# One layer of a hybrid decoder on one core: the second half of x read already turned, row roots and C A^t sums moved from GpSimd to VectorE, the last chunk's stores moved to ScalarE's queue

## The chip, the cores and the metric

The kernel runs on one core of one Trainium2 chip. The core has five engines that work beside each other, each through its own instruction queue in order: TensorE (PE; its weight loads are shown as PEld), VectorE (DVE), ScalarE (ACT), GpSimd (POOL) and SyncE (SP), which does no arithmetic and issues most DMAs. ACT issues some DMAs too. An instruction that waits for a semaphore holds up all that stands behind it in the same queue; a queue's own entries are shown as SPq, ACTq and so on.

The metric is device microseconds (us) of one execution. Lower is better.

## The reference

One layer (DEPTH = 1) over 2048 tokens of width 1024, in float32:

```
h = rms_norm(x, norm1_g)
proj = h @ w_in                       # columns shared by three mixers
o_a = swa_sink_mixer(qa, ka, va)      # attention, window 128
o_b = s5_mixer(u)                     # complex diagonal state space, 512 columns u of proj
o_c = nsa_mixer(qc, kvc, gates)       # compressed, selected and window attention
x = x + rms_norm_each(o_a, o_b, o_c) @ w_out
x = x + relu(rms_norm(x) @ w_up)**2 @ w_down
```

The RMS norm divides each row of x by the root of its mean square. The kernel applies this factor after the product, row by row, and the gain norm1_g to the weights. Of s5_mixer only one thing matters here: for each of 32 groups the kernel needs C A^t for t = 0 to 16, a complex product whose two halves are multiplied apart and summed.

## The kernel before, in words

The kernel is five stages behind each other: the front (norm, w_in, the state space), attention A beside the GLU of the state space, the sparse attention with the output product, the up projection and the down projection. The change lies in the front (`phase_front`, the first 420 us).

**Rows.** The 2048 tokens are cut into 16 row tiles s = 0 to 15 of 128 tokens each (tokens s, s + 16, ...). The host hands x over as it is. `fetch(s)` (L101) loads tile s, 128x1024 float32 or 512 KB, on SP's queue. `load_h(s)` (L106) turns it in: eight transposes of 128x128 on PE (L116), four to a PSUM tile pt with two buffers; ACT casts pt to float32r (hh, L118), DVE makes the remainder hl = pt - hh (L119). `scale()` (L121) squares x in place on ACT with a sum (L123) and takes the reciprocal root of the sum on POOL by `rsqrt_into`, eight instructions on 128x1 (L44 to L49: two to start, three rounds of two). This factor r is called the row root below. Tile s of x has three buffers; hh and hl have eight, so row tiles 8 to 15 take the place of 0 to 7.

**Products.** A `chunk` is the product of eight row tiles (half 0: s = 0 to 7; half 1: s = 8 to 15) with one slice of w_in: a, b, c (384, 384 and 396 columns) and u, v (256 columns each, together the state space's u). One row's `product` (L155) is 24 matmuls: eight steps of three, high by high, low by high, high by low (L76 to L78), into one of two PSUM accumulators pm. For u and v ACT evicts pm to u_st with the row root as scale (L172). For a, b, c ACT evicts to a row buffer po (L176), squares the heads (L178), DVE sums them (L179), and the row is stored to memory (L180) on SP's queue, one row late (`store(1)`). Weights come on SP's queue (L133) and are split by ACT (L141) and DVE (L142).

**Order around the change.** A first list of steps does half 0 of a. A second one merges half 0 of b, c and u with `ssm_tables`, which makes the tables of the state space; its last PE work is the turning of C (p, L452). The third one (L236 to L244) is where the change lies: half 0 of v, half 1 of v, half 1 of u, 24 products; after every second entry from the third on one `turn_in(s)` for s = 8 to 15 is inserted (load_h, scale, and the fetch of s + 3); x8 to x10 are fetched ahead of it; and this list is merged with the 17 steps of `pair_steps`. A fourth one does half 1 of a, b and c (each row in two parts) merged with `ssm_steps`, the scan. Then the next stage begins, with its weights (graw, L626) and bias tables (Ts, T).

**Pairs.** Step b of `pair_steps` makes C A^t for two groups: oCA = AR * C1 on POOL (L483), ot = AI * C2 on DVE (L484, one buffer), and the sum oCA + ot on POOL (L485). Then for the pair before: its oCA is stored (L489), two small products pk on PE (L493), and kst, with one buffer, is filled by DVE (L496) and ACT (L497) and stored (L498).

The lists give the order of the program. A planner beneath places each instruction on its engine's queue from that order and from when it expects it to be ready: the trace shows fetches of the second half at 35.77 to 45.76 us, long before their place in the lists. Memory of a pool that has been closed can be given to a later pool, whose first use then waits for the last use of the earlier one.

Of the kernel before, what the change touches and what calls it, by code (L numbers as in the profile page):

```python
# [7 lines left out]
F32 = mybir.dt.float32  # L8
# [8 lines left out]
P = 128  # L17
# [39 lines left out]
def rsqrt_into(nc, pool, y, ss, scale, n, tag, eng=None):  # L57
    h = pool.tile([P, n], F32, tag=tag + "h", name=tag + "h")
    t = pool.tile([P, n], F32, tag=tag + "t", name=tag + "t")
    rsqrt_steps(eng or nc.vector, y, ss, h, t, scale)  # L60
# [17 lines left out]
    nc.tensor.matmul(out, sl, mh, start=False, stop=last)  # L78


def phase_front(tc, C, x, norm1_g, w_in, u_st, pd, rh_a, prm, dkp, dca, pre, extra, done):

    nc = tc.nc
    with ExitStack() as ctx:
# [11 lines left out]
        pdv = {kind: t.rearrange("(c s) e -> s c e", s=T16) for kind, t in pd.items()}  # L96
        wv = w_in[0].rearrange("(k p) n -> p k n", p=P)
        g1 = sm.tile([P, NK], F32, tag="g1", name="g1", bufs=1)
        r_of, raw_x, hs = {}, {}, {}

        def fetch(s):  # L101
            if s < T16:
                raw_x[s] = xp.tile([P, D], F32, tag="x", name=f"x{s}", bufs=3)
                nc.sync.dma_start(raw_x[s], xv[s])

        def load_h(s):  # L106
            xt = raw_x.pop(s)
            p = hp[s % 8 == 7]
            hh = p.tile([P, NK, P], F32R, tag="hh", name=f"hh{s}")
            hl = p.tile([P, NK, P], F32R, tag="hl", name=f"hl{s}")  # L110
            hs[s] = hh, hl
            for half in range(2):
                pt = ps_t.tile([P, 4, P], F32, tag="pt", name=f"pt{s}_{half}")
                for j in range(4):
                    k = 4 * half + j
                    nc.tensor.transpose(pt[:, j], xt[:, k * P:(k + 1) * P], C["ident"])  # L116
                sl = slice(4 * half, 4 * half + 4)
                nc.scalar.copy(hh[:, sl], pt)  # L118
                nc.vector.tensor_tensor(hl[:, sl], pt, hh[:, sl], op=ALU.subtract)  # L119

            def scale():  # L121
                ss = xp.tile([P, 1], F32, tag="ss", name=f"ss{s}")
                nc.scalar.activation(xt, xt, AF.Square, accum_out=ss)  # L123
                r = r_of[s] = sm.tile([P, 1], F32, tag="r", name=f"r{s}", bufs=T16)
                rsqrt_into(nc, xp, r, ss, 1.0 / D, 1, "rq", nc.gpsimd)
            return scale

        def raw_w(ch, q, m, pool, bufs):
# [26 lines left out]
        def product(s, W, ch, k0=0, k1=NK, between=()):  # L155
            kind, c0, n = ch
            hh, hl = hs[s]
            if k0 == 0:
                open_[s, ch] = ps_m.tile([P, n], F32, tag="pm", name=f"pm{s}_{kind}{c0}")
            pm = open_[s, ch]  # L160
            between = list(between)
            for k in range(k0, k1):
                mm3(nc, pm, hh[:, k], hl[:, k], W[k][0], W[k][1], k == 0, k == NK - 1)
                if between:
                    between.pop(0)()
            if k1 < NK:
                return
            if kind == "u":
                r = T16 - 1 - s
                g0 = (c0 - 512) // 16  # L170
                dst = u_st[:, g0:g0 + 16, (r // 8) * P + (r % 8) * 16:(r // 8) * P + (r % 8) * 16 + 16]
                nc.scalar.activation(dst, pm.rearrange("p (g q) -> p g q", q=16), AF.Copy, scale=r_of[s])  # L172
            else:
                f, nh, step = HEADS[kind]
                o = sp.tile([P, n + nh], F32, tag="po", name=f"po{s}_{kind}", bufs=3)
                nc.scalar.activation(o[:, 0:n], pm, AF.Copy, scale=r_of[s])  # L176
                sq = sp.tile([P, 6, 64], F32, tag="sq", name=f"sq{s}_{kind}", bufs=1)[:, 0:nh]
                nc.scalar.activation(sq, o[:, f:f + nh * step].rearrange("p (h d) -> p h d", d=step)[:, :, 0:64], AF.Square)  # L178
                nc.vector.tensor_reduce(o[:, n:n + nh], sq, axis=AX.X, op=ALU.add)  # L179
                rows.append(lambda: nc.sync.dma_start(pdv[kind][s], o))  # L180
                store(1)

        rows = []
# [50 lines left out]
        run(merge(body, [lambda: next(gen, None)] * TABLE_PARTS))  # L234
        pairs = pair_steps(tc, C, S, dkp, dca, pre, ps_g)
        body = chunk(ch_v, 0, W[0, ch_v], []) + chunk(ch_v, 1, W[0, ch_v], steps[1, ch_u]) + chunk(ch_u, 1, W[1, ch_u], steps[1, ch_a])  # L236
        for s in range(8, 11):
            fetch(s)
        for s in range(8, T16):
# [2 lines left out]
                fetch(s + 3)  # L242
            body.insert(2 * (s - 8) + 3, turn_in)
        run(merge(body, pairs))  # L244
        done()
        tp = ctx.enter_context(tc.tile_pool(name="sg", bufs=2))
        c_b = chunk(ch_b, 1, W[1, ch_b], steps[1, ch_c], 2)
# [224 lines left out]
def pair_steps(tc, C, S, dkp, dca, tp, ps):  # L472

    nc = tc.nc
    M = {}
    NB = G // GB

    def outer(b):
        bc = [P, GB, 17, 16]
        CA = M[b] = tp.tile(bc, F32, tag="oCA", name=f"oCA{b}", bufs=2)  # L480
        t1 = tp.tile(bc, F32, tag="ot", name=f"ot{b}", bufs=1)
        ar, ai = (S[n][:, :, group_slice(b)].rearrange("p t g -> p g t").unsqueeze(3).broadcast_to(bc) for n in ("AR", "AI"))
        nc.gpsimd.tensor_tensor(CA, ar, S["C1"][:, group_slice(b)].unsqueeze(2).broadcast_to(bc), op=ALU.mult)  # L483
        nc.vector.tensor_tensor(t1, ai, S["C2"][:, group_slice(b)].unsqueeze(2).broadcast_to(bc), op=ALU.mult)  # L484
        nc.gpsimd.tensor_tensor(CA, CA, t1, op=ALU.add)  # L485

    def local(b):
        CA = M.pop(b)
        nc.sync.dma_start(dca[b], CA)  # L489
        pk = ps.tile([P, GB, 256], F32, tag="pb", name=f"pk{b}", bufs=2)  # L490
        for i in range(GB):
            g = b * GB + i
            nc.tensor.matmul(pk[:, i], S["Yp"][:, g:g + 8].rearrange("p a b -> p (a b)"), CA[:, i, 0:16].rearrange("p a b -> p (a b)"),  # L493
                             start=True, stop=True)
        kst = tp.tile([16, GB, 256], F32, tag="kst", name=f"kst{b}", bufs=1)
        nc.vector.tensor_tensor(kst[:, :, 0:16], pk[0:16, :, 0:16], S["dD"][:, group_slice(b)], op=ALU.add)  # L496
        nc.scalar.copy(kst[:, :, 16:256], pk[0:16, :, 16:256])  # L497
        nc.sync.dma_start(dkp[group_slice(b), :, 112:368].rearrange("g q c -> q g c"), kst)  # L498

    return [lambda b=b: (b < NB and outer(b), b and local(b - 1)) for b in range(NB + 1)]  # L500
# [1318 lines left out]
                w = nw  # L1819


def trunk(tc, x, norm1_g, w_in, qk_g, sinks, rel_bias, a_re, a_im, log_dt, b_re, b_im, c_re, c_im, d_skip, glu_w, glu_b,
          cmp_pos, cmp_w1, cmp_w2, out_norm_g, w_out, norm2_g, w_up, w_down,
          k_ident, k_anti, k_ramp, k_oh2, k_ohs, k_blk, k_forced, k_wmask, k_rows31, out, dbg=None):
    nc = tc.nc
    with ExitStack() as ctx:
# [9 lines left out]
        def late_loads(tp, ps):  # L1836
# [7 lines left out]
            for j in (0, 2):  # L1844
# [17 lines left out]
        u_st = up.tile([P, G, 256], F32, name="u_st")  # L1862
        c_pre = c_all.enter_context(ExitStack())
        pre = c_pre.enter_context(tc.tile_pool(name="pre", bufs=1, side="right"))
        phase_front(tc, C, x, norm1_g, w_in, u_st, pd, rh_a, (a_re, a_im, log_dt, b_re, b_im, c_re, c_im, d_skip), dkp, dca,
                    pre, late_loads, c_pre.close)
        c_b = c_all.enter_context(ExitStack())
        bp = c_b.enter_context(tc.tile_pool(name="bp", bufs=1, reuse_waits="tile"))
# [90 lines left out]
```

## Time and profile before

| | us |
|---|---|
| median of 3 runs | 2546.9 (2543.54 to 2548.43) |
| profiled execution | 2552.13 |
| its span | 2550.2 |
| PE busy | 2444.3 (96%) |
| DVE busy | 1721.8 (68%) |
| ACT busy | 1324.6 (52%) |
| POOL busy | 1203.2 (47%) |

The profile is of one execution. A group or a row names the line of the kernel (L116), the engine, the operation, out<-in by the program's names without buffer numbers, and partitions x elements. In an order of time the first two columns are the start and the length in us, and in brackets stands the idle time of the engine before it and what ended it. Rows of one kind that follow each other are merged (x8). Matmuls are pipelined and their ends are modelled, so starts say more than lengths. A row of the waits reads: who waited, for whom, us in total, times, longest.

The stages by time: half 0 of the products until about 163 us, the rows 8 to 15 turned in from 163 to 209, the rest of u until 240, the fourth list until 417, then the other stages.

### The profile page before, as it was taken

The page shows a single profiled execution, that of the slowest core. Times are in us where ns is not written, and L with a number is a line of the kernel's source. Part 1 is how long each engine was busy: PE and PEld are TensorE (multiplying, and loading weights), DVE is VectorE, ACT ScalarE, POOL GpSimd, SP SyncE. Part 2 cuts the span into 40 slices and gives each one's busy share as a digit, 9 for nine tenths or more (in the row PEclk, how much of TensorE's full clock was granted, in tenths as well). Part 3 has the DMA queues.
Part 4 walks back from the last instruction along what each step waited for, and adds up shares of the span by engine and source line. Part 5 has one row for each costly group of instructions (what it writes and reads, how often), then busy time and mean ns, then how long its engine had stood idle before and what let it go on. Part 6 is the DMA issues. An engine that isn't in the chain of part 4 may idle for free.

```text
span 2550.2 us, 38303 instructions
## 1 busy us (share of the span) xinstructions
PE 2444.3 (96%) x12776; PEld 2065.4 (81%) x12776; DVE 1721.8 (68%) x3424; ACT 1324.6 (52%) x2767; POOL 1203.2 (47%) x1263
## 2 busy tenths in 40 slices
PE   8999999899989999899999999999999999999999
PEld 8989997677778878788778787788887888888887
DVE  4743884775587787677554545745457888888886
ACT  6334545675576566555455555654554444334442
POOL 3045222223445354454646666666554444545447
PEclk9999999998999999999999999999999999999999
DMA  6153425311121112131656677755547534444335
GB/s 200 61 127 96 125 87 163 97 58 49 44 92 51 57 51 68 55 98 55 198 193 189 191 198 210 227 160 155 148 121 261 164 102 126 133 132 132 120 101 197
DMA packets 397174, 324.65 MB, mean 127 GB/s; under 512 B 51974, under 2 KB 363916, under 8 KB 395152
## 3 DMA queue, kind: packets, MB, share of 16 engines
q1 hardware_dynamic: 360880, 297.03, 39.2%
q10 hardware_dynamic: 36096, 25.17, 3.1%
q8 instruction: 101, 1.65, 0.3%
q14 instruction: 97, 0.79, 0.1%
HBM read 209.66 MB, written 112.45 MB: 126 GB/s over the span
## 4 chain that ended last, share of the span: by engine, by line
PE 63%; DVE 5%; DMA 3%; POOL 3%; issue 3%; ACT 2%; SPq 0%; ACTq 0%; DVEq 0%; POOLq 0%
PE pdc L1755 7%; PE pdb L1755 7%; PE pda L1755 7%; PE pub L1566 6%; PE puc L1566 6%; PE pua L1566 6%; PE pdd L1755 3%; PE pud L1566 3%; PE poc L911 3%; PE pps L900 2%; PE pw L76 2%; PE pw L77 2%; PE pw L78 2%; PE pqs L876 1%; PE pqs L877 1%
## 5 line engine op out<-in xcount | busy, mean ns | idle before, releaser
L1420 ACT CAST v<-vr 128x512 fp32r<-128x512 f32 x224 | 139.4, 624 | 305.4 <-DMA vr<-vd 142.9
L1421 DVE TENSOR_TENSOR v<-vr,v 128x512 fp32r<-128x512 f32 x224 | 233.7, 1052 | 78.2 <-ACT v L1420 77.9
L1755 PE MATMUL pdc<-dw,v 128*128 128x512 f32 x768 | 187.4, 393 | 4.1 <-ACT dw L1420 3.2
L1755 PE MATMUL pda<-dw,v 128*128 128x512 f32 x768 | 184.5, 389 | 0.0
L1755 PE MATMUL pdb<-dw,v 128*128 128x512 f32 x768 | 184.5, 389 | 0.0
L1537 POOL TENSOR_TENSOR fs<-ur,ur 128x512 f32<-128x512 f32 x64 | 92.9, 1452 | 176.4 <-DMA ur<-in_w_up 131.2
L1755 PEld LDWEIGHTS pdc<-dw,v 128*128 128x128 f32 x768 | 145.5, 190 | 35.8 <-ACT dw L1420 3.6
L1755 PEld LDWEIGHTS pdb<-dw,v 128*128 128x128 f32 x768 | 144.2, 188 | 30.0
L1755 PEld LDWEIGHTS pda<-dw,v 128*128 128x128 f32 x768 | 144.1, 188 | 30.0
L1421 DVE TENSOR_TENSOR ul<-ur,uh 128x512 fp32r<-128x512 f32 x96 | 93.3, 972 | 109.8 <-ACT uh L1420 109.7
L1421 DVE TENSOR_TENSOR ul<-fs,uh 128x512 fp32r<-128x512 f32 x128 | 133.7, 1048 | 33.9 <-ACT uh L1420 33.9
L1420 ACT CAST uh<-fs 128x512 fp32r<-128x512 f32 x128 | 78.2, 621 | 141.7 <-PE pub L1566 56.4
L887 POOL TENSOR_SCALAR sls<-sls,dens,gt 128x128 f32<-128x128 f32 (+15 forms) x64 | 81.7, 1277 | 105.8 <-DVE dens L886 85.7
L903 ACT CAST ths<-pps 128x512 fp32r<-128x512 f32 (+1 forms) x144 | 79.8, 560 | 79.6 <-PE poc L911 58.1
L904 DVE TENSOR_TENSOR tls<-pps,ths 128x512 fp32r<-128x512 f32 (+1 forms) x144 | 93.8, 658 | 38.7 <-ACT ths L903 34.1
L76 PE MATMUL pw<-wo_h,mh 128*128 128x512 f32 x256 | 109.7, 428 | 7.6 <-ACT mh L1250 5.8
L900 PE MATMUL pps<-c_ident,sls 128*128 128x128 f32 x544 | 103.0, 281 | 9.1 <-POOL sls L887 5.4
L1582 POOL TENSOR_TENSOR ev<-e,e 128x512 f32<-128x512 f32 x64 | 98.3, 1535 | 27.9 <-ACT e L1579 16.8
L887 POOL TENSOR_SCALAR slw<-slw,denw,gt 128x640 f32<-128x640 f32 (+4 forms) x64 | 52.9, 827 | 122.1 <-DVE denw L886 98.5
L78 PE MATMUL pw<-wo_h,ml 128*128 128x512 f32 x256 | 105.0, 411 | 2.1 <-DVE ml L1251 2.1
L77 PE MATMUL pw<-wo_l,mh 128*128 128x512 f32 x256 | 106.4, 416 | 0.0
L1566 PE MATMUL puc<-fh,uh 128*128 128x512 f32 x256 | 101.0, 395 | 5.3 <-DVE eu L1575 5.3
(562 smaller groups left out, 7960.6 us busy)
## 6 DMA issues: line engine op xcount, KB each, us to landing
vr<-vd SPq DMA_DIRECT2D x224, 256.0 KB
ur<-in_w_up SPq DMA_DIRECT2D x128, 256.0 KB
vd<-ev SPq DMA_DIRECT2D x128, 256.0 KB
vd<-e ACTq DMA_DIRECT2D x64, 256.0 KB
dr<-in_w_down SPq DMA_DIRECT2D x32, 512.0 KB
x<-in_x SPq DMA_DIRECT2D x16, 512.0 KB
mx<-in_x SPq DMA_DIRECT2D x16, 512.0 KB
x<-mx ACTq DMA_DIRECT2D x16, 512.0 KB
```

The lines of the kernel that those rows point to most:

```text
L76: nc.tensor.matmul(out, sh, mh, start=first, stop=False)
L77: nc.tensor.matmul(out, sh, ml, start=False, stop=False)
L78: nc.tensor.matmul(out, sl, mh, start=False, stop=last)
L887: nc.gpsimd.tensor_scalar(x, x, den[:, h:h + 1], gate, op0=ALU.mult, op1=ALU.mult)
L900: nc.tensor.transpose(pt[:, j, hh], sls[hh][:, (b0 + j) * P:(b0 + j + 1) * P], C["ident"])
L904: nc.vector.tensor_tensor(tl[:, 0:nb], pt[:, 0:nb], th[:, 0:nb], op=ALU.subtract)
L1420: nc.scalar.copy(dh, src)
L1421: nc.vector.tensor_tensor(dl, src, dh, op=ALU.subtract)
L1537: nc.gpsimd.tensor_tensor(t, x, y, op=op)
L1566: nc.tensor.matmul(bank[b], w[:, k], h[o][:, k], start=first and k == 0 and n == 0, stop=k == HALF - 1 and n == 2, skip_group_check=True)
L1582: nc.gpsimd.tensor_tensor(tile_("v" + o), x, y, op=op)
L1755: nc.tensor.matmul(bank[b, q], x[:, q, j], y[:, j], start=first and j == 0 and n == 0, stop=j == 1 and n == 2, skip_group_check=True)
```

## The change

Four edits:

1. For s = 8 to 15 the host hands over a second input x_t with the tiles already turned. `fetch` loads it (xt, 512 KB, three buffers) ahead of x, and `load_h` casts from it in SBUF; the transposes and pt are not used for these rows. x itself is still loaded, for the square, now with two buffers in place of three.
2. Both lie in a new pool a_x2, opened after the tables and closed ahead of `done()`.
3. The row root of s = 8 to 15 and the sum of C A^t in every pair are on DVE in place of POOL.
4. The stores of chunk c for s = 8 to 15 are issued by ACT in place of SP.

```
         def fetch(s):
             if s < T16:
-                raw_x[s] = xp.tile([P, D], F32, tag="x", name=f"x{s}", bufs=3)
+                if s >= 8:
+                    turned_x[s] = late_p[0].tile([P, NK, P], F32, tag="xt", name=f"xt{s}", bufs=3)
+                    nc.sync.dma_start(turned_x[s], xt_in[s - 8])
+                raw_x[s] = (late_p[0] if s >= 8 else xp).tile([P, D], F32, tag="x", name=f"x{s}", bufs=2 if s >= 8 else 3)
                 nc.sync.dma_start(raw_x[s], xv[s])
...
-                pt = ps_t.tile([P, 4, P], F32, tag="pt", name=f"pt{s}_{half}")
-                for j in range(4):
-                    k = 4 * half + j
-                    nc.tensor.transpose(pt[:, j], xt[:, k * P:(k + 1) * P], C["ident"])
                 sl = slice(4 * half, 4 * half + 4)
+                if s >= 8:
+                    pt = turned_x[s][:, sl]
+                else:
+                    pt = ps_t.tile([P, 4, P], F32, tag="pt", name=f"pt{s}_{half}")
+                    for j in range(4):
+                        k = 4 * half + j
+                        nc.tensor.transpose(pt[:, j], xt[:, k * P:(k + 1) * P], C["ident"])
                 nc.scalar.copy(hh[:, sl], pt)
                 nc.vector.tensor_tensor(hl[:, sl], pt, hh[:, sl], op=ALU.subtract)
...
-                rsqrt_into(nc, xp, r, ss, 1.0 / D, 1, "rq", nc.gpsimd)
+                rsqrt_into(nc, xp, r, ss, 1.0 / D, 1, "rq", nc.vector if s >= 8 else nc.gpsimd)
...
-                rows.append(lambda: nc.sync.dma_start(pdv[kind][s], o))
+                rows.append(lambda: (nc.scalar if s >= 8 and kind == "c" else nc.sync).dma_start(pdv[kind][s], o))
...
+        c_x = ctx.enter_context(ExitStack())
+        late_p.append(c_x.enter_context(tc.tile_pool(name="a_x2", bufs=1)))
         for s in range(8, 11):
             fetch(s)
...
         run(merge(body, pairs))
+        c_x.close()
         done()
...
-        nc.gpsimd.tensor_tensor(CA, CA, t1, op=ALU.add)
+        nc.vector.tensor_tensor(CA, CA, t1, op=ALU.add)
...
+            host["x_t"] = _np.asarray(inputs[n])[0].reshape(P, T16, NK, P).transpose(1, 3, 2, 0)[8:]
```

More of the change, by code (lines that the diff above doesn't have):

```diff
@@ L78, in mm3, with phase_front @@
     nc.tensor.matmul(out, sl, mh, start=False, stop=last)
-def phase_front(tc, C, x, norm1_g, w_in, u_st, pd, rh_a, prm, dkp, dca, pre, extra, done):
+def phase_front(tc, C, x, xt_in, norm1_g, w_in, u_st, pd, rh_a, prm, dkp, dca, pre, extra, done):
     nc = tc.nc
@@ L98, in phase_front @@
         g1 = sm.tile([P, NK], F32, tag="g1", name="g1", bufs=1)
-        r_of, raw_x, hs = {}, {}, {}
+        r_of, raw_x, turned_x, hs, late_p = {}, {}, {}, {}, []
         def fetch(s):
             if s < T16:
-                raw_x[s] = xp.tile([P, D], F32, tag="x", name=f"x{s}", bufs=3)
+                if s >= 8:
+                    turned_x[s] = late_p[0].tile([P, NK, P], F32, tag="xt", name=f"xt{s}", bufs=3)
+                    nc.sync.dma_start(turned_x[s], xt_in[s - 8])
+                raw_x[s] = (late_p[0] if s >= 8 else xp).tile([P, D], F32, tag="x", name=f"x{s}", bufs=2 if s >= 8 else 3)
                 nc.sync.dma_start(raw_x[s], xv[s])
@@ L1819, in phase_down, with trunk @@
                 w = nw
-def trunk(tc, x, norm1_g, w_in, qk_g, sinks, rel_bias, a_re, a_im, log_dt, b_re, b_im, c_re, c_im, d_skip, glu_w, glu_b,
+def trunk(tc, x, x_t, norm1_g, w_in, qk_g, sinks, rel_bias, a_re, a_im, log_dt, b_re, b_im, c_re, c_im, d_skip, glu_w, glu_b,
           cmp_pos, cmp_w1, cmp_w2, out_norm_g, w_out, norm2_g, w_up, w_down,
@@ L1864, in trunk @@
         pre = c_pre.enter_context(tc.tile_pool(name="pre", bufs=1, side="right"))
-        phase_front(tc, C, x, norm1_g, w_in, u_st, pd, rh_a, (a_re, a_im, log_dt, b_re, b_im, c_re, c_im, d_skip), dkp, dca,
+        phase_front(tc, C, x, x_t, norm1_g, w_in, u_st, pd, rh_a, (a_re, a_im, log_dt, b_re, b_im, c_re, c_im, d_skip), dkp, dca,
                     pre, late_loads, c_pre.close)
@@ L1947 @@
     arrays, args = {}, []
-    host = {n: inputs[n] for n in _INS}
+    host = {}
+    for n in _INS:
+        host[n] = inputs[n]
+        if n == "x":
+            host["x_t"] = _np.asarray(inputs[n])[0].reshape(P, T16, NK, P).transpose(1, 3, 2, 0)[8:]
     host.update(_shape_constants())
```

## The prediction

> **What bounds the kernel now.** I read the page first, then the busy time by stretches of the span, then the instructions of the changed stage in order of time, engine by engine. Durations come from one profiled execution: its span is 2550.2 us and its own time 2552.1 us, 5.2 us above the median of 2546.9 us of the runs. I work out a difference inside the trace and take it off the median.
>
> ```profile
> span 2550.2 us, 38303 instructions
> PE 2444.3 (96%) x12776; PEld 2065.4 (81%) x12776; DVE 1721.8 (68%) x3424; ACT 1324.6 (52%) x2767; POOL 1203.2 (47%) x1263
> ```
>
> TensorE (PE) fills 96% of the span, so by the page only less PE work shortens anything. The front, up to 420 us, must be read by stage. In the view by stretches the columns are the stretch, its length, busy us and instructions of PE, PEld, DVE, ACT and POOL, granted clock, DMA share and GB/s.
>
> ```profile
> 0.00:20.00 20.00, 12.85 (x60) 12.06 (x61) 8.81 (x22) 12.14 (x22) 5.69 (x20) 1.00 0.78 246
> 144.00:163.00 19.00, 19.00 (x160) 18.92 (x159) 7.99 (x14) 6.65 (x15) 5.47 (x4) 1.00 0.36 109
> 163.00:209.00 46.00, 41.54 (x316) 38.89 (x315) 17.62 (x33) 23.22 (x48) 38.72 (x72) 1.00 0.36 112
> 209.00:240.00 31.00, 30.75 (x241) 29.80 (x240) 10.93 (x18) 11.41 (x25) 18.49 (x21) 1.00 0.36 112
> 260.00:300.00 40.00, 39.91 (x252) 38.40 (x251) 34.24 (x72) 22.65 (x48) 11.73 (x10) 1.00 0.32 96
> 300.00:350.00 50.00, 48.80 (x308) 46.98 (x307) 46.18 (x101) 26.14 (x57) 12.80 (x11) 1.00 0.41 117
> ```
>
> From 163 to 209 us the second half's x is turned in. PE is full just before and just after; here it is busy 41.54 of 46 us. GpSimd (POOL) is busy 38.72 us there, more than in any stretch beside it. Its order of time shows why:
>
> ```profile
> 181.45 0.72 POOL L44 TENSOR_SCALAR rqh<-ss 128x1 f32<-128x1 f32 x1
> ...
> 184.84 1.17 POOL L483 TENSOR_TENSOR oCA<-k_AR,k_C 128x544 f32<-128x544 f32 x1
> 186.09 1.33 POOL L485 TENSOR_TENSOR oCA<-oCA,ot 128x544 f32<-128x544 f32 x1
> 187.51 0.72 POOL L44 TENSOR_SCALAR rqh<-ss 128x1 f32<-128x1 f32 x1
> ```
>
> One cycle of POOL, eight small instructions of a row root and the two halves of a C A^t product, takes 187.51 - 181.45 = 6.06 us, without a wait in it. The others queue behind it; the waits of this stretch are
>
> ```profile
> DVE ot L484 <- POOL oCA L485: 23.4, 8, 4.1
> ACT kst L497 <- DVE kst L496: 17.8, 7, 5.5
> ```
>
> VectorE (DVE) waits for POOL's sum, ScalarE (ACT) for DVE's kst, and behind kst on ACT stands the eviction that frees PE's accumulator. One cycle of PE, cut from its order of time:
>
> ```profile
> 185.34 1.04 PE L116 MATMUL pt<-c_ident,x 128*128 128x128 f32 x8
> 186.22 1.03 PE L493 MATMUL pk<-oCA,k_Y 128*128 128x256 f32 x4
> ...
> 189.81 0.28 PE L78 MATMUL pm_u<-wh_u,hl 128*128 128x256 f32 x1
> 190.51 0.66 PE L116 MATMUL pt<-c_ident,x 128*128 128x128 f32 x4 [0.43 <-DVE hl L119]
> ```
>
> Starts are to be read here, since modelled ends overlap. Eight transposes hold PE from 185.34 to 186.22, 0.88 us. A pair's product and one row's product hold it from 186.22 to the start of the last matmul at 189.81 and about 0.12 us for that one (24 matmuls share some 3 us), 3.71 us. The stretch holds eight sets of transposes and nine of the other: 8 x 0.88 + 9 x 3.71 = 7.0 + 33.4 = 40.4 us. So 5.6 of the 46 us are waits, more than the busy column admits. The stage is paced by POOL; the rest of the front by PE.
>
> **The change, part by part.** *Transposes.* All 64 of s = 8 to 15 leave PE, 7.0 us, and with them the wait of a transpose for its PSUM tile (0.43 us in the last row). If nothing else paced the stage, it would fall from 46 to 33.4 us, a gain of 12.6 us. That is the upper end.
>
> *POOL's work.* Per cycle the row root and the sum go; 1.17 us of 6.06 is left, and POOL paces nothing. What is late next is DVE, which takes both.
>
> ```profile
> 178.21 1.67 DVE L484 TENSOR_TENSOR ot<-k_AI,k_C 128x544 f32<-128x544 f32 x1 [4.08 <-POOL oCA L485]
> ...
> 181.40 0.72 DVE L484 TENSOR_TENSOR ot<-k_AI,k_C 128x544 f32<-128x544 f32 x1 [0.32 <-POOL oCA L485]
> ```
>
> The sum on DVE has the shape of ot and two SBUF inputs like it: 0.72 us, at worst the 1.33 us that POOL needs; I take 0.72, the same engine and shape. For the row root there is a DVE row elsewhere in the kernel, the same eight instructions on 128x1:
>
> ```profile
> 1260.19 0.15 DVE L44 TENSOR_SCALAR nqh<-ns 128x1 f32<-128x1 f32 x1 [0.64 <-ACT mix L939]
> ...
> 1262.31 0.47 DVE L941 TENSOR_SCALAR mix<-oc,nr 128x256 f32<-128x256 f32 x1
> ```
>
> From its start to the next instruction it holds DVE 2.1 us. DVE in the 46 us then has 17.62 + 8 x 0.72 + 8 x 2.1 = 40.2 us to do, more than PE's 33.4. Paced by DVE alone the stage gains 46 - 40.2 = 5.8 us. That is the lower end as long as DVE is kept busy.
>
> Which end is nearer? DVE isn't tied to this stretch: r is wanted only when a row's first product is evicted, and the casts no longer wait for PE, so turn-ins can start in the 19 us before, where DVE is busy 7.99. Over 144 to 209 us DVE has 7.99 + 17.62 + 10 x 0.72 (two of the sums lie in the first 19 us, where POOL's four instructions are two products and two sums) + 8 x 2.1 = 49.6 us. In the two later stretches DVE runs 34.24 of 40 (86%) and 46.18 of 50 (92%) while PE stays at 98 to 100%. At 92% the 65 us become 53.9, at 86% 57.7: a gain of 11.1 or 7.3. I take the mean, **9.2 us**, also the middle of 5.8 and 12.6.
>
> *Casts.* hh on ACT and hl on DVE keep their number and shape and read SBUF in place of PSUM; costed at nothing, since ACT is busy 23.22 of 46 us. hl thereby becomes an instruction with two SBUF inputs, which counts in a rival below.
>
> *Loads.* SyncE's queue (SP) gets eight more issues and 4 MB. More weighs when they start:
>
> ```profile
> 45.76 0.33 SPq L104 DMA_DIRECT2D x<-in_x  x1
> ...
> 144.27 1.04 PE L452 MATMUL p<-c_ident,craw 128*128 128x128 f32 x8
> ...
> 156.30 0.91 ACT L141 ACTIVATE wh_u<-wr_u,g 128x256 fp32r<-128x256 f32 x2 [1.93 <-DMA wr_u<-in_w_in]
> ```
>
> Before, x10, the third of the second half, is asked for at 45.76 us, more than 100 us ahead of its use. The new pool is opened after the tables; if it lies on their memory, its loads can start only when the tables' last readers are through, the transposes of craw at 144.27. Then five loads of 512 KB, 2.6 MB, come at once, at the 246 GB/s of the first 20 us until about 155. They pass ahead of the weights that ACT waits for at 156.30, behind which an eviction stands. PE's two accumulators cover about a product. The cost is 0 if the memory is free earlier, 4 us if the weights come that much later; I take 0.7, since SP may place the weights first. With x in two buffers, x(s+3) also waits on SP for the square of s+1 instead of s, and behind it stand that cycle's stores of CA and kst, on which the next use of kst's single buffer waits. With 512 KB landing in 2.1 us at that rate, a cycle of 4 to 5 us hides it.
>
> *Stores of the last chunk.* Eight issues go from SP to ACT.
>
> ```profile
> 399.78 7.70 SPq L180 DMA_DIRECT2D pc<-po_c  x2
> 407.53 0.91 SPq L626 DMA_DIRECT2D graw<-in_glu_w  x2
> ...
> 413.99 0.38 SPq L719 DMA_DIRECT2D Ts<-rs  x1
> ```
>
> The second store of the first row waits on SP until 407, and the next stage's loads (graw, then Ts) stand behind it. PE pays later:
>
> ```profile
> 419.25 1.10 PE L712 MATMUL bpfs<-Ts,c_anti 128*128 128x512 f32 x2 [2.18 <-DMA Ts<-rs]
> ```
>
> Earlier loads win at most these 2.2 us, and nothing if their memory isn't free; I take 1.0. An issue costs ACT
>
> ```profile
> 1248.04 0.33 ACTq L1268 DMA_DIRECT2D x<-mx  x1
> ```
>
> 0.33 us, 2.6 us for eight, beside product streams of over 4 us per row and part; the second accumulator hides it, and without it 2.6 us would be paid. The Trainium skill (DMA: Bandwidth & Descriptors, section "Issuing engines are not separate DMA queues") says that transfers issued from different engines share the same 16 DMA engines, so that another issuer saves only sequencer time. By it the store move would bring nothing of its own and the total would be 1.0 us less; here the SP rows show an issue standing for a semaphore, which isn't bandwidth.
>
> **Sum.** 9.2 - 0.7 + 1.0 = 9.5 us off. From 240 to 420 us PE is paced by its own products, and the stages behind start when it gets there, so I let the gain pass through whole: 2552.1 becomes 2542.6 in the profiled frame, and 2546.9 becomes **2537.4 us**. With the ends of the main term (7.3 to 11.1) this case spans about 2535.5 to 2539.5, with all terms at their ends 2532 to 2545.
>
> **Rivals.** *PE paces everything*: the order of DVE's work is loose enough, all 12.6 us come, and the border gives 2.2: 14.8 off, 2532.1 us. For it: DVE idles half of 144 to 163 us. Against: 40.2 us of DVE work beside 33.4 of PE.
>
> *Slower: a ring through ACT and DVE.* The row root on DVE waits for ACT's square, and if it stands ahead of the pair's work in DVE's queue, the cycle closes on itself:
>
> ```profile
> 188.35 0.55 ACT L497 COPY kst<-pk 16x480 f32<-16x480 f32 x1 [3.15 <-issue]
> ...
> 191.07 0.19 ACT L123 ACTIVATION_READ_ACCUMULATOR x<-x 128x1 f32 x1
> ```
>
> From kst on ACT at 188.35 the square's sum is out at 191.26, 2.9 us later. Add row root 2.1, ot 0.72, sum 0.72, and some 0.25 for kst on DVE: 6.7 us, above POOL's 6.06. Eight cycles lose 5.1 us; with the other terms 4.8, so 2551.7 us, and with ot blocked as at 178.21 (0.95 more each) up to 2559. It decides when the cycle passes 6.06 us. For it: the waits above have the eviction behind kst today. Against: the row root can be queued behind the pair's work, and the cycle is then DVE's own 5 us.
>
> *The shared port: no gain.* The ot at 178.21 took 1.67 us, the one at 181.40 0.72; the first ran while POOL, by its order of time, had a product under way. Now sum and hl have two SBUF inputs too. If each of POOL's eight products blocks one DVE instruction by 0.95 us, DVE has 40.2 + 7.6 = 47.8 us to do, 1.8 more than the stage takes now: 2546.9 + 1.8 - 0.3 = 2548.4 us. The Trainium skill (SBUF — State Buffer, section "Who interferes with whom") states this as a lock between a DVE instruction with two SBUF inputs and a GpSimd instruction that reads SBUF; the 1.67 us row agrees. Against: POOL runs 1.17 us per cycle, and DVE would often be in its small instructions then.
>
> *Late loads*: the weights come 4 us late: 9.2 - 4 + 1.0 = 6.2 off, 2540.7 us.
>
> **How the numbers follow.** Forecast 0.44, PE paces 0.16, late loads 0.14, shared port 0.14, ring 0.12. About 0.2% (5 us) is what a measurement of this kernel can tell, so faster means under 2541.8: the forecast, the first rival and more than half of the late loads, 0.68. Slower means over 2552.0: most of the ring and the bad end of the port, 0.10. The rest, 0.22, is the same. The range, 2530 to 2549 us, takes in the first rival and the port, and leaves out the ring and gains beyond 17 us.
>
> **What would show it.** In the changed profile: no L116 after 163 us; POOL's only instruction per cycle is L483; DVE over 80% busy across the turned-in rows; the last u_st product some 9 us before 240; graw issued on SP without waiting behind a pc store, and the wait of bpfs for Ts shorter. I am wrong if u_st evictions stand behind kst or a cast that waits for xt by more than 2 us per cycle, if ot and the sum are mostly near 1.67 us, or if the lead at 240 us is gone by 430.

## The result, and the profile after

The changed kernel takes 2533.65 us (median, 2531.87 to 2535.41), the one before in the same runs 2547.66 us. The ratio is 0.9943, with a 95% interval of 0.9922 to 0.9965: faster by about 14 us (8.9 to 19.9 by the interval), where 9.5 were forecast. The profiled execution's span falls from 2550.2 to 2531.2 us.

The page of the changed kernel, first rows:

```profile
span 2531.2 us, 38164 instructions
PE 2430.6 (96%) x12712; PEld 2053.3 (81%) x12712; DVE 1742.9 (69%) x3504; ACT 1327.1 (52%) x2767; POOL 1163.1 (46%) x1183
```

PE has 64 instructions fewer and is still at 96%: the shares of the page tell nothing of where 19 us went. The busy time by stretches does (columns as in the prediction):

```profile
163.00:209.00 46.00, 42.90 (x312) 41.16 (x311) 34.97 (x93) 23.20 (x47) 13.40 (x11) 0.96 0.58 191
160.00:200.00 40.00, 36.90 (x264) 35.26 (x263) 35.47 (x95) 22.97 (x46) 11.87 (x9) 0.96 0.68 226
```

In the stage of the turned-in rows POOL falls from 38.72 to 13.40 us and DVE rises from 17.62 to 34.97. From 160 to 200 us DVE is busy 35.47 of 40 us, 89%. PE gains little busy time in the 46 us (41.54 to 42.90), but none of it is a transpose now.

How far the front is ahead is read at the last eviction of u_st, the end of the third list. From the order of time on ACT, the first and the last eviction before, then after:

```profile
130.91 0.47 ACT L172 ACTIVATE u_st<-pm_u,r 128x256 f32<-128x256 f32 x1 [1.92 <-PE pm_u L78]
...
249.55 0.47 ACT L172 ACTIVATE u_st<-pm_u,r 128x256 f32<-128x256 f32 x1
```
```profile
129.62 0.48 ACT L178 ACTIVATE u_st<-pm_u,r 128x256 f32<-128x256 f32 x1 [1.92 <-PE pm_u L78]
...
240.22 0.47 ACT L178 ACTIVATE u_st<-pm_u,r 128x256 f32<-128x256 f32 x1
```

The last comes 9.3 us earlier. (The prediction and the text ahead of it end this list at 240 us before the change; by these rows it ended at 249.55.) 1.3 us of the 9.3 can't be put down to the change: the first eviction of u, ahead of the rows that are turned in, stood at 130.91 us before and at 129.62 after, and lies between 129.4 and 131.5 us in all traces of this study. So the length from the first to the last eviction of u is the better reading, 118.6 us before and 110.6 after: 8.0 us. The next place is the first matmul of the compression (cph), before and after:

```profile
500.10 3.84 PE L766 MATMUL cph<-cX,cw 128*128 128x129 f32 x32
```
```profile
484.17 3.84 PE L775 MATMUL cph<-cX,cw 128*128 128x129 f32 x32
```

From the last u_st to it 6.6 us more are won. The other 3 us of the span come later, in stages that the change doesn't touch.

PE's largest wait left in the stage stands in its order of time:

```profile
176.02 1.10 PE L502 MATMUL pk<-oCA,k_Y 128*128 128x256 f32 x4 [2.56 <-DVE r L49]
```

It is taken up with the experiments. The next stage's loads on SP, after:

```profile
385.03 0.95 SPq L635 DMA_DIRECT2D graw<-in_glu_w  x2
...
402.59 0.38 SPq L728 DMA_DIRECT2D Ts<-rs  x1
```

graw is asked for 22.5 us earlier than before (407.53), Ts 11.4 us earlier (413.99), although the stage itself starts 9.6 us earlier only (last eviction of po_c at 416.7 and 407.1).

### The profile page after: what moved, and what is told of

The parts are those of the page before. It is cut to its first block, busy times and chain, and to the rows that moved or that the text cites. A ratio compares the mean times of both kernels' runs of the same rounds, so it can differ in the third digit from the quotient of the medians.

```text
span 2531.2 us, 38164 instructions
## 1 busy us (share of the span) xinstructions
PE 2430.6 (96%) x12712; PEld 2053.3 (81%) x12712; DVE 1742.9 (69%) x3504; ACT 1327.1 (52%) x2767; POOL 1163.1 (46%) x1183
## 4 chain that ended last, share of the span: by engine, by line
PE 65%; DVE 5%; POOL 3%; DMA 2%; issue 2%; ACT 2%; SPq 0%; ACTq 0%; DVEq 0%; POOLq 0%
PE pub L1575 7%; PE pdc L1764 7%; PE pdb L1764 7%; PE pda L1764 7%; PE puc L1575 7%; PE pua L1575 6%; PE pdd L1764 3%; PE pud L1575 3%; PE poc L920 3%; PE pw L76 2%; PE pps L909 2%; PE pw L77 2%; PE pw L78 2%; PE pqs L885 1%; DVE sls L888 1%
## 5 line engine op out<-in xcount | busy, mean ns | idle before, releaser
L1575 PE MATMUL pua<-fh,uh 128*128 128x512 f32 x256 | 101.5, 397 | 3.3 <-ACT e L1595 3.3
```

Of the source, the lines that this page charges most:

```text
L1575: nc.tensor.matmul(bank[b], w[:, k], h[o][:, k], start=first and k == 0 and n == 0, stop=k == HALF - 1 and n == 2, skip_group_check=True)
```

## The experiments

Theory: three terms make the time. POOL paces the turned-in rows, and mainly its row roots matter there; the transposes count once POOL has let go; the stores on ACT free SP's queue. Rivals: PE's work alone, the loads, the port that DVE and POOL share. Ratios are to the kernel before, run on the same chip, with 95% intervals. In the traces two lengths are read, in us: A from the first to the last eviction of u, B from there to the first cph.

| | stores of c | A | B | ratio |
|---|---|---|---|---|
| before | SP | 118.6 | 250.6 | |
| after | ACT | 110.6 | 244.0 | 0.9943 |
| 1 row roots on POOL | ACT | 119.4 | 244.6 | 0.9991 |
| 2 sums on POOL | ACT | 113.3 | 244.1 | 0.9969 |
| 3 turned x alone | SP | 124.2 | 247.2 | 1.003 |
| 4 DVE moves alone | SP | 114.1 | 248.2 | 0.999 |
| 5 stores on SP | SP | 112.9 | 251.9 | 0.9968 |
| 6 stores on ACT alone | ACT | 120.3 | 244.7 | 0.9986 |
| 7 third x | ACT | 110.7 | 243.1 | 0.9932 |
| 8 third oCA | ACT | 108.5 | 243.2 | 0.9915 |
| 9 all late stores on ACT | ACT | 112.5 | 247.6 | 0.9941 |
| 10 as 3, transposes kept idle | SP | 124.0 | 247.6 | 1.0032 |
| 11 third x and third oCA | ACT | 109.0 | 242.7 | 0.9932 |
| 12 as 3, hl from PSUM | SP | 120.4 | 250.5 | 0.9998 |

A and B are of one execution each. Runs 5 and 9 have the code of the changed kernel up to the late stores and an A of 112.9 and 112.5 against 110.6, so a difference of 2 us in A proves nothing by itself; the ratios decide, the lengths say where. Where the intervals of two ratios overlap widely, the two kernels aren't told apart.

**1. Row roots back on POOL**, the rest as changed.

```
-  rsqrt_into(nc, xp, r, ss, 1.0 / D, 1, "rq", nc.vector if s >= 8 else nc.gpsimd)
+  rsqrt_into(nc, xp, r, ss, 1.0 / D, 1, "rq", nc.gpsimd)
```

> The changed kernel with the row roots of s = 8 to 15 back on POOL; the sums of C A^t stay on VectorE. Read by the end of the turning-in stage, the last u_st eviction (249.6 us before, 240.2 us changed). Theory (the stage is freed when POOL's cycle falls below PE's need): POOL has 6.06 - 1.33 = 4.7 us per cycle against PE's 3.7, VectorE is freed of 2.1 per cycle, so the stage ends 0 to 4 us later than in the changed kernel, at 240 to 244 us, total 0.998 to 1.000 of changed + 4 us. Rival (both moves are needed, since the ring of POOL, VectorE and ScalarE stays as long as POOL holds the row roots): back to about 248 us. Rival (only the 7.0 us of transposes count): no difference to the changed kernel.

0.9991 (0.9981 to 1.0001). A is 119.4 us, as long as before the change; the last eviction of u comes at 249.7 us, where 240 to 244 were expected. The stretch in its trace, and one group of POOL in it (total busy, mean ns of one):

```profile
163.00:209.00 46.00, 36.12 (x246) 33.78 (x245) 23.91 (x42) 21.09 (x43) 34.74 (x58) 0.93 0.55 182
```
```profile
L48 POOL TENSOR_SCALAR rqt<-r,rqh 128x1 f32<-128x1 f32 x18 | 12.2, 680 | 1.8
```

POOL is busy 34.74 us of the 46 again, PE only 36.12. Without transposes and without the sums on POOL, the stage gains nothing as long as the row roots stay there. What the expectation had wrong is their length: it took the cycle as 4.7 us, with the row root as long as before, where L48 had a mean of 341 ns; here it is 680 ns, and a cycle in which POOL doesn't wait lasts 6.09 us (the products at 177.24 and 183.33). What holds these small instructions up is the subject of run 12.

**2. Sums of C A^t back on POOL.**

```
-  nc.vector.tensor_tensor(CA, CA, t1, op=ALU.add)
+  nc.gpsimd.tensor_tensor(CA, CA, t1, op=ALU.add)
```

> The changed kernel with the sums of C A^t back on POOL; the row roots of s = 8 to 15 stay on VectorE. POOL has 1.17 + 1.33 = 2.5 us per cycle and VectorE 0.72 less. Theory (POOL's load no longer paces, VectorE is near the pace): the stage ends within 2 us of the changed kernel's 240.2 us, rather earlier than later. Rival (the sum must be on VectorE, since ot on VectorE waits for POOL's sum and holds up kst): 243 to 247 us.

0.9969 (0.9954 to 0.9983), A 113.3 us. The list ends at 243.5 us, 3.3 later than in the changed kernel, where the theory had allowed 2 and the rival began at 243. With 2 us of scatter in A, and with a ratio whose interval overlaps that of the change (0.9922 to 0.9965), this run doesn't decide between them. Next to run 1 it says that of the two moves to DVE that of the sums is the smaller one.

**3. The turned x alone**: row roots, sums and stores as before.

```
-  rsqrt_into(nc, xp, r, ss, 1.0 / D, 1, "rq", nc.vector if s >= 8 else nc.gpsimd)
+  rsqrt_into(nc, xp, r, ss, 1.0 / D, 1, "rq", nc.gpsimd)
...
-  rows.append(lambda: (nc.scalar if s >= 8 and kind == "c" else nc.sync).dma_start(pdv[kind][s], o))
+  rows.append(lambda: nc.sync.dma_start(pdv[kind][s], o))
...
-  nc.vector.tensor_tensor(CA, CA, t1, op=ALU.add)
+  nc.gpsimd.tensor_tensor(CA, CA, t1, op=ALU.add)
```

> The kernel before with the turned x alone: no transposes for s = 8 to 15, but row roots, sums and stores where they were. Theory (POOL paces this stage with 6.06 us per cycle): of the 7.0 us of transposes almost nothing comes back; the stage ends at 246 to 249.6 us and the total is within 4 us of before. Rival (PE at 96% paces, so what leaves PE is gained): the stage ends at 241 to 243 us, total 7 us or more under before.

1.003 (1.0019 to 1.0041): slower than before by some 7.6 us, with 64 matmuls less, where a time within 4 us of before was expected. A is 124.2 us, 5.6 longer, and the list ends at 253.8 us (246 to 249.6 expected). Why is the subject of runs 10 and 12.

**4. The two DVE moves alone**: transposes and stores as before.

```
-  rsqrt_into(nc, xp, r, ss, 1.0 / D, 1, "rq", nc.gpsimd)
+  rsqrt_into(nc, xp, r, ss, 1.0 / D, 1, "rq", nc.vector if s >= 8 else nc.gpsimd)
...
-  nc.gpsimd.tensor_tensor(CA, CA, t1, op=ALU.add)
+  nc.vector.tensor_tensor(CA, CA, t1, op=ALU.add)
```

> The kernel before with the two moves to VectorE alone: transposes stay on PE, x as before, stores on SP. Theory: PE needs 40.4 of the 46 us, VectorE 40.2; the stage ends 2 to 5 us earlier than before, at 244.5 to 247.5 us. Rival (a ring of cast, square, row root and kst through ScalarE and VectorE): 250 us or later, total slower than before. Rival (POOL alone was the cause): 241 us or less.

0.999 (0.9978 to 1.0003), so in the whole time a gain isn't clear. A is 4.5 us shorter, the list ends at 243.6 us (244.5 to 247.5 expected), and by the busy time by stretches nothing is left in the stage but PE:

```profile
163.00:209.00 46.00, 46.00 (x362) 44.75 (x361) 37.48 (x110) 25.93 (x53) 11.76 (x10) 1.00 0.41 126
```

PE is busy all 46 us. The prediction read 5.6 us of waits out of the matmul starts where the busy column leaves 4.46; A gains 4.5, which with its scatter fits both. DVE does 37.48 us of work here without holding PE up.

**5. Stores of c back on SP**, the rest as changed, and **6. the stores on ACT alone**, the rest as before.

```
-  rows.append(lambda: (nc.scalar if s >= 8 and kind == "c" else nc.sync).dma_start(pdv[kind][s], o))
+  rows.append(lambda: nc.sync.dma_start(pdv[kind][s], o))
```
```
-  rows.append(lambda: nc.sync.dma_start(pdv[kind][s], o))
+  rows.append(lambda: (nc.scalar if s >= 8 and kind == "c" else nc.sync).dma_start(pdv[kind][s], o))
```

> The changed kernel with the last chunk's stores back on SP's queue. The front does the same; read by the first matmul of the next stage's bias table (419.3 us before, 407.3 changed), by the first matmul of the compression (500.1 before, 484.2 changed) and by when SP issues the first GLU weights (407.5 before, 385.0 changed). Theory (the freed SP queue lets the next stage's loads go ahead, and the wait for them is gone): the table starts 2 to 3 us later than in the changed kernel, the compression 4 to 7 us later, the total is 2 to 7 us more. Rival (the lead behind 410 us is chance of the clock or of the planner's order): the table starts within 1 us of 407.3 and the total is the same as the changed kernel's.

> The kernel before with the last chunk's stores on ScalarE's queue and nothing else. Theory (a queue freed): the first GLU weights are issued some 13 us earlier than in the kernel before, the table starts 2 to 3 us earlier (416.5 to 417.5 us), the total falls by 2 to 7 us. Rival (the stores matter only with the shorter front, or not at all): total within 1 us of before. Rival (the eight issues of 0.33 us hold up ScalarE's evictions): total 1 to 3 us more.

Run 5: 0.9968 (0.9958 to 0.9979); run 6: 0.9986 (0.9975 to 0.9997). So the eight stores are worth 0.14% alone (3.6 us, 0.8 to 6.4). On top of the rest the two ratios differ by 0.25% (0.9968 to 0.9943, 6.4 us), but their intervals overlap, so by the times alone this may be anything from about 0 to 12 us. They were put at 1.0 us. The order of time of run 5 shows the price on SP's queue, then on PE:

```profile
394.08 7.71 SPq L186 DMA_DIRECT2D pc<-po_c  x2
401.84 2.38 SPq L635 DMA_DIRECT2D graw<-in_glu_w  x2
...
409.62 0.38 SPq L728 DMA_DIRECT2D Ts<-rs  x1
```
```profile
415.26 1.95 PE L721 MATMUL bpfs<-Ts,c_anti 128*128 128x512 f32 x2 [3.88 <-DMA Ts<-rs]
...
457.05 2.07 PE L721 MATMUL bpf<-T,c_anti 128*128 128x512 f32 x2 [2.18 <-DMA T<-r]
```

Two stores stand on SP for 7.7 us together, graw, Ts and T go out behind them, and PE waits 3.88 us for Ts and 2.18 for a T. B says the same: 247.2 to 251.9 us in the six traces with these stores on SP (mean 249.3), 242.7 to 244.7 in seven of the eight with them on ACT (mean 243.8). The eighth is run 9's 247.6, an execution with a mean granted clock of 0.966 where the changed kernel had 0.987. In run 5 the compression starts 11.7 us later than in the changed kernel, where 4 to 7 were expected; 3.8 of this are there already at the last eviction of u. In run 6 graw is asked for 11.6 us and the bias table started 1.0 us earlier than before (13 and 2 to 3 expected).

**7. Three buffers for the late x**, and **8. three buffers for oCA**, both on the changed kernel. Two stalls were to be told apart: x(s+3) waiting on SP, and the wait of pk at 176 us.

```
-  raw_x[s] = (late_p[0] if s >= 8 else xp).tile([P, D], F32, tag="x", name=f"x{s}", bufs=2 if s >= 8 else 3)
+  raw_x[s] = (late_p[0] if s >= 8 else xp).tile([P, D], F32, tag="x", name=f"x{s}", bufs=3)
```
```
-  CA = M[b] = tp.tile(bc, F32, tag="oCA", name=f"oCA{b}", bufs=2)
+  CA = M[b] = tp.tile(bc, F32, tag="oCA", name=f"oCA{b}", bufs=3)
```

> The changed kernel with three buffers for x of s = 8 to 15 in place of two, so that a load of x waits on SP for the square two rows earlier and not for the next one. Theory (the loads' wait on SP for a square also holds up the store of oCA behind it): the 6.9 us of POOL at 174 us shrink, the stage ends 1 to 3 us earlier than 240.2. Rival (the wait is in the transfers and not in the queue: 1 MB of x per row at the 277 GB/s of 170 to 180 us): no difference, or later, since more is asked for at once.

> The changed kernel with three buffers for oCA in place of two. In the changed kernel PE still stands 2.56 us at 176 us for a pair's product, behind the sum on VectorE, behind POOL's product, which starts at 173.96 after 6.9 us of idle time, and the granted clock falls to 0.85 in 170 to 180 us. Theory (POOL waits for the second buffer, whose store of 272 KB lies behind two loads of x of 512 KB each): with a third buffer this wait goes, and the clock with it; the stage ends 2 to 4.5 us earlier, at 236 to 238 us. Rival (VectorE is the pace, its 8 to 9.5 busy us of every 10): the stage ends within 1 us of 240.2.

Run 7: 0.9932 (0.9918 to 0.9946), and the stall of pk is still there, 2.7 us. Run 8: **0.9915 (0.9901 to 0.993), 2527.7 us**, the lowest of all, with an A of 108.5 and the list's end at 238.1 us (236 to 238 expected); its interval overlaps that of the change (0.9922 to 0.9965) a little, so that the total is lower is likely and not shown. The stretch around the stall, by stretches, in the changed kernel and in run 8:

```profile
170.00:180.00 10.00, 7.44 (x46) 7.08 (x46) 8.43 (x32) 5.57 (x11) 2.85 (x2) 0.85 0.86 277
```
```profile
170.00:180.00 10.00, 9.59 (x72) 9.10 (x71) 9.65 (x34) 6.92 (x15) 2.70 (x2) 1.00 0.90 299
```

72 matmuls in place of 46, and a granted clock of 1.00 in place of 0.85. The profile had put PE's wait down to a row root (DVE r L49), and POOL's wait ahead of it to another; neither feeds pk. What ended late must have been the store of an earlier oCA: of that buffer's two readers the other, pk on PE, had started at 168.50. From the changed kernel's order of time, POOL and SP:

```profile
173.96 1.16 POOL L492 TENSOR_TENSOR oCA<-k_AR,k_C 128x544 f32<-128x544 f32 x1 [6.88 <-DVE rqt L48]
```
```profile
169.76 0.42 SPq L498 DMA_DIRECT2D dca<-oCA  x1
170.23 0.43 SPq L105 DMA_DIRECT2D xt<-in_x_t  x1
170.71 1.87 SPq L107 DMA_DIRECT2D x<-in_x  x1
```

The store goes out at 169.76 with two loads of 512 KB behind it, and POOL's product into that buffer starts 4.2 us later. It is late already: the sum that it stores was through at 164.7, and it stood on SP behind the store of a kst, issued at 169.39. With a third buffer the stall is gone (runs 8 and 11); a third x alone leaves it (run 7). That the loads are what makes the store slow was not tried.

**9. All stores of the second half on ACT, 11. both third buffers at once.**

```
-  rows.append(lambda: (nc.scalar if s >= 8 and kind == "c" else nc.sync).dma_start(pdv[kind][s], o))
+  rows.append(lambda: (nc.scalar if s >= 8 else nc.sync).dma_start(pdv[kind][s], o))
```

> The changed kernel with all stores of half 1 on ScalarE's queue, chunks a and b too. Theory (the last chunk's stores matter because the next stage's first loads stand behind them; behind a and b stand only loads of weights, CA and Wc that are early enough): within 2 us of the changed kernel, and 16 more issues of 0.33 us on ScalarE where it is half busy. Rival (any wait of a store on SP costs): 2 to 5 us less.

> The changed kernel with both third buffers, oCA and x of s = 8 to 15. A third oCA alone ended the stage at 238.1 us (240.2 changed), a third x alone at 241.1. Theory (only the store of oCA held POOL; a third x buffer asks for loads earlier and buys nothing): within 1.5 us of the third oCA alone, 2526 to 2529 us. Rival (both waits are on SP's queue and add up): 1.5 us or more under the third oCA alone.

Run 9: 0.9941 (0.992 to 0.9962), not told apart from the change. That fits the expectation, by which only the last chunk's stores stand ahead of the next stage's loads; intervals of this width don't exclude the rival's 2 to 5 us. Run 11 (the two edits of 7 and 8): 0.9932 (0.9918 to 0.9946), 2528.7 us, no better than run 8 alone.

**10. The turned x alone, with PE kept busy.** A first theory for run 3 was the clock: in its trace the granted clock is 0.90 to 0.91 from 163 to 220 us, where the kernel before has 1.00. So the 64 transposes were put back into run 3 as work whose result nothing reads. The stretch in run 3, and then in run 10:

```profile
163.00:180.00 17.00, 12.19 (x78) 11.32 (x77) 5.46 (x9) 9.75 (x19) 14.78 (x28) 0.90 0.68 229
```
```profile
163.00:180.00 17.00, 15.06 (x113) 13.87 (x112) 6.51 (x11) 8.24 (x16) 15.19 (x23) 1.00 0.66 217
```

```
+  pt = ps_t.tile([P, 4, P], F32, tag="pt", name=f"pt{s}_{half}")
+  for j in range(4):
+      k = 4 * half + j
+      nc.tensor.transpose(pt[:, j], xt[:, k * P:(k + 1) * P], C["ident"])
   if s >= 8:
       pt = turned_x[s][:, sl]
```

> The run with the turned x alone (row roots and sums on POOL, stores on SP), with the 64 transposes of s = 8 to 15 put back as work whose results nothing reads; casts still come from the turned tile. The turned x alone made the kernel 0.3% slower and its stage ended at 253.8 us against 249.6 before, with the granted clock at 0.90 to 0.91 from 163 to 220 us. Theory (with POOL as the pace, PE stands more once the transposes are gone, the clock is taken down, and the products that remain run slower): with the transposes back the clock is 1.0 for most of the stage, and it ends at 248 to 251 us, total within 0.1% of before. Rival (the 4 MB of loads and the waits on SP are what costs): it ends at 253 us or later, total as with the turned x alone or slower.

1.0032 (1.0021 to 1.0042), and A is 124.0 us all the same. The theory missed, but the run is no clean test of it. The granted clock is back at 1.00 from 163 to 180 us only (0.92 and 0.91 in the 40 us behind), and the idle transposes brought a wait of their own on PE:

```profile
PE pt L120 <- DMA x<-in_x: 6.4, 4, 2.2
```

What the trace does say is that POOL's cycle didn't shorten: the row roots at 189.19 and 196.28 us are 7.09 us apart, without a wait between them.

**12. The turned x alone, but hh and hl read PSUM again.** Run 3's trace held another lead. First DVE and POOL of the kernel before, in order of time, then both of run 3:

```profile
183.71 1.29 DVE L119 TENSOR_TENSOR hl<-pt,hh 128x512 fp32r<-128x512 f32 x2 [1.50 <-ACT hh L118]
```
```profile
184.17 0.34 POOL L48 TENSOR_SCALAR rqt<-r,rqh 128x1 f32<-128x1 f32 x1
```
```profile
187.57 0.73 DVE L493 TENSOR_TENSOR ot<-k_AI,k_C 128x544 f32<-128x544 f32 x1 [4.57 <-POOL oCA L494]
188.21 1.29 DVE L125 TENSOR_TENSOR hl<-xt,hh 128x512 fp32r<-128x512 f32 x2
```
```profile
180.93 1.43 POOL L48 TENSOR_SCALAR rqt<-r,rqh 128x1 f32<-128x1 f32 x1
...
187.52 1.43 POOL L48 TENSOR_SCALAR rqt<-r,rqh 128x1 f32<-128x1 f32 x1
```

Before, hl takes one input from PSUM, and POOL's small instructions pass beside it, L48 in 0.34 us. In run 3 hl reads xt and hh, both in SBUF; while ot and two hl run from 187.57 to 189.4, POOL's L48 lasts 1.43 us. From 180.93 to 187.52 is one cycle of POOL without a wait in it: 6.59 us, against 6.06 before. (Before, too, one small instruction was held up: L44 took 0.72 us at 187.51, beside an ot from 187.46 to 188.18, and takes 0.19 in run 3 where no such instruction runs.) To test this, ACT first copies xt to the PSUM tile, and hh and hl read it there.

```
+  pt = ps_t.tile([P, 4, P], F32, tag="pt", name=f"pt{s}_{half}")
   if s >= 8:
-      pt = turned_x[s][:, sl]
+      nc.scalar.copy(pt, turned_x[s][:, sl])
```

> The turned x alone (row roots, sums and stores as before), with one thing added: ACT first copies the turned tile into the PSUM tile pt, and the cast hh and the remainder hl read pt there as they did before the change, so hl has one SBUF input instead of two. ACT does 16 more copies of about 0.6 us, 10 us over the 46. Theory: with the turned x alone POOL still paces the stage, and its cycle is longer (6.6 against 6.06 us) because two hl instructions with two SBUF inputs hold its small instructions up: L48 has a mean of 597 ns there against 341 before, L45 298 against 190. Then here POOL's small instructions are back near 341 and 190 ns, the cycle is near 6.06 us where POOL has no wait, the last u_st eviction comes at about 249 to 251 us instead of 253.8, and the ratio to the kernel before falls from 1.003 to about 1.000 or below. Rival: the late and doubled loads or the use of the buffers pace it; then the last u_st eviction stays at 253 us or later and the ratio at 1.003, and the longer work of ACT could make it worse, whatever POOL's small instructions show.

0.9998 (0.9983 to 1.0013), where run 3 had 1.003 (1.0019 to 1.0041). A falls from 124.2 to 120.4 us. POOL's groups over 163 to 209 us, in the kernel before, in run 3 and in run 12 (total busy, mean ns of one):

```profile
L48 POOL TENSOR_SCALAR rqt<-r,rqh 128x1 f32<-128x1 f32 x21 | 7.2, 341 | 2.1
```
```profile
L48 POOL TENSOR_SCALAR rqt<-r,rqh 128x1 f32<-128x1 f32 x18 | 10.7, 597 | 1.4
```
```profile
L48 POOL TENSOR_SCALAR rqt<-r,rqh 128x1 f32<-128x1 f32 x18 | 7.6, 420 | 1.6
```

And run 12's cycle, by the starts of its row roots:

```profile
164.94 0.72 POOL L44 TENSOR_SCALAR rqh<-ss 128x1 f32<-128x1 f32 x1
...
171.00 0.72 POOL L44 TENSOR_SCALAR rqh<-ss 128x1 f32<-128x1 f32 x1
...
177.08 0.72 POOL L44 TENSOR_SCALAR rqh<-ss 128x1 f32<-128x1 f32 x1
```

6.06 and 6.08 us again in these first cycles; the later ones vary. PE's waits from 129 to 255 us, in run 3 and in run 12:

```profile
PE pk L502 <- POOL oCA L494: 9.6, 5, 3.1
```
```profile
PE pk L502 <- ACT kst L506: 6.0, 2, 3.0
PE pk L502 <- POOL oCA L494: 5.6, 5, 2.1
```

In run 3 PE waits for POOL's sums in cycle after cycle, and in run 12 by 4.0 us less, of which 2.8 come back as waits for kst (3.2 us in run 3). So hl from SBUF holds up POOL's row roots and lengthens the cycle that PE waits for, and with hl back on PSUM the loss against before is gone. The Trainium skill (SBUF — State Buffer, section "Who interferes with whom") says that a DVE instruction with two SBUF inputs and a GpSimd instruction that reads SBUF exclude each other, and that issue order, not the shape, decides which of them waits; these rows agree, and here the small instructions of POOL are those that wait. Some 0.5 us in each of eight or nine cycles would be 4 to 5 us of the 5.6 by which A had grown, and 3.8 came back. That all of the 3.8 is the port is not shown. The granted clock from 180 to 220 us is 0.99 and 1.00 in run 12, where run 3 has 0.91. By the starts of the matmuls, 32 of run 3 and 6 of run 12 follow each other at 0.21 us in place of 0.12: some 3 us and 0.6, as an estimate of the most that the lower clock can have cost. The edit also moves hh's input, which was not tried apart.

## Why the prediction was right, point by point

**The pace.** "The stage is paced by POOL" held: with the row roots on POOL nothing is gained (run 1). The main term of 9.2 us, less 0.7 for the loads, was 8.0 us in A (5.7 and 6.1 in runs 5 and 9), and run 5, all but the stores, is at 0.9968, 8.2 us (5.4 to 10.7). The parts don't add: the DVE moves alone give 0.1% (run 4, not clear of nothing), and the turned x, a loss of 0.3% alone, gives 0.22% behind them (run 4 to run 5).

The size of the term owes something to luck. It was worked out with DVE as the next pace, at 86 to 92% busy. DVE's work came as counted, 49.86 us from 144 to 209 against 49.6, and from 160 to 200 us it is busy 89%; but over the whole 65 us it is 77%. That DVE sets the pace isn't shown: with the sums taken off it again (run 2; DVE busy 30.68 us from 163 to 209 in place of 34.97) A is no shorter, and the largest wait that PE had left was for a buffer (run 8).

**The mis-sized term** is the stores: "Earlier loads win at most these 2.2 us ... I take 1.0". The times put them at 3.6 us alone and 6.4 with the rest, with intervals that both still take in 1.0; B, shorter by 5 us in the mean with the stores on ACT, puts them above the bound. The bound took one wait, that of bpfs for Ts, as all that stood behind SP. That wait is gone, but PE waits for T as well: its waits for Ts and T together were 2.2 + 2.4 = 4.6 us before, 6.1 in run 5, 2.9 in run 6 and 2.8 after (rows of before, then of after):

```profile
PE bpf L712 <- DMA T<-r: 2.4, 2, 2.0
PE bpfs L712 <- DMA Ts<-rs: 2.2, 1, 2.2
```
```profile
PE bpf L721 <- DMA T<-r: 2.8, 2, 2.6
```

That explains 1.7 to 3.3 us. Much of the rest goes with the granted clock, of which the prediction said nothing at this place. From 400 to 500 us, in the kernel before and then in the changed one:

```profile
400.00:500.00 100.00, 86.28 (x464) 66.96 (x462) 65.81 (x201) 64.35 (x191) 25.79 (x26) 0.93 0.49 136
```
```profile
400.00:500.00 100.00, 88.21 (x523) 68.07 (x522) 73.90 (x231) 72.81 (x224) 28.65 (x29) 0.98 0.54 148
```

It is 0.93 in run 5 too and 0.98 in run 6. But runs 3, 4 and 10, with the stores on SP, have 0.97 to 0.98 there, and the shortest B of their kind, 247.2 to 248.2, where run 12, at 0.91, has 250.5. So by the means of these few traces some 4 us go with the queue, and about 3 more appear only where the clock fell as well; why it fell in those executions stays open.

The Trainium skill (DMA: Bandwidth & Descriptors, section "Issuing engines are not separate DMA queues") was quoted against this edit: another issuer saves only sequencer time. The rows of run 5 and B show more than that: what was saved isn't bandwidth, but the time that later loads stood behind a store that waits in an in-order queue.

**The rivals.** *PE paces everything* did not come: PE still waits in the stage, and run 8 shows that its largest wait there could be had too. *Late loads* came as a fact, not as a price. From the changed kernel's order of time on SP:

```profile
144.16 0.33 SPq L105 DMA_DIRECT2D xt<-in_x_t  x1
```

The first xt is asked for at 144.16 us, when craw's last transposes are through; ACT waited 1.9 us for an xt and, from 150 to 240 us, for no weight of u. The stall of pk at 176 us may be an indirect price of the loads; that was not tried. *The ring through ACT and DVE* did not close: pair work and row roots alternate in DVE's queue. *The shared port* on DVE was rare. The groups of the changed kernel from 144 to 209 us:

```profile
L125 DVE TENSOR_TENSOR hl<-xt,hh 128x512 fp32r<-128x512 f32 x16 | 12.2, 772 | 3.2 <-ACT hh L124 3.2
L494 DVE TENSOR_TENSOR oCA<-oCA,ot 128x544 f32<-128x544 f32 x13 | 11.0, 850 | 7.6 <-POOL oCA L492 6.9 <-DVE ot L493 0.5
L493 DVE TENSOR_TENSOR ot<-k_AI,k_C 128x544 f32<-128x544 f32 x13 | 9.7, 747 | 0.1
```

Single rows show both cases of hl, held up for 1.29 us (166.32) and free at 0.68 (167.97).

Means of 772, 850 and 747 ns against 0.68 us for a free hl and 0.72 for the other two make 3.5 us over the 42 instructions, where the rival needed 7.6. But "costed at nothing", said of the casts, is near the truth only because the same change takes the row roots off POOL. Where they stay, the cost falls on POOL (runs 1 and 3). The slower case that the prediction should have named is this one, the port with POOL as the one that waits.

**What stays open**, beside that clock and the part that it has in run 12: the 3 us of the span behind the compression's start, in code that is the same. Whether the doubled loads cost run 3 anything beside the port was not tried by itself.

## What to carry to other kernels

Taking work from an engine that is 96% busy gained nothing here in a stage that another engine paces, and lost where the substitute reads SBUF and PSUM was read before, since a VectorE instruction with two SBUF inputs then held up GpSimd's (POOL's cycle 6.06 to 6.59 us). First take the pace away, then the work; alone, each edit moves the time by 0.3% at most (1.003, 0.999, 0.9986), and together they gave 0.9943. Price an issue that stands on an in-order queue by every load behind it, not by the first wait that the profile shows; and a wait put down to an instruction that feeds nothing may be a buffer that has not come free.

## What was not expected of the hardware

- POOL's 128x1 instruction took 0.34 us undisturbed and 1.43 us beside an ot and an hl with two SBUF inputs (run 3); beside hl with one input in PSUM it took 0.34 (before).
- The eight instructions of a row root hold POOL 3.4 us of its 6.06 us cycle (181.45 to 184.84), some 0.5 of it in an L44 held up beside ot; on DVE in the changed kernel they are busy 0.14 + 0.15 + 3 x 0.27 + 3 x 0.21 = 1.7 us, by its order of time:

```profile
170.06 0.14 DVE L44 TENSOR_SCALAR rqh<-ss 128x1 f32<-128x1 f32 x1
170.23 0.15 DVE L45 TENSOR_SCALAR r<-rqh 128x1 int32<-128x1 int32 x1
170.42 0.27 DVE L48 TENSOR_SCALAR rqt<-r,rqh 128x1 f32<-128x1 f32 x1
170.73 0.21 DVE L49 TENSOR_SCALAR r<-rqt,r 128x1 f32<-128x1 f32 x1
```

- PE waiting 2.56 us once went with a granted clock of 0.85 over the ten us around; without the wait it was 1.00 (run 8). A low busy share alone doesn't bring this: in the kernel before, PE is as little busy in the same ten us, at 1.00:

```profile
170.00:180.00 10.00, 7.42 (x54) 6.48 (x52) 3.80 (x6) 3.74 (x8) 8.35 (x13) 1.00 0.40 118
```

- Transposes put back as idle work went with a clock of 1.00 in place of 0.90 over the 17 us from 163 on, and with no gain in time (run 10).
